# The lower halves of 56 weight chunks: by an accumulating transfer instead of a subtraction on VectorE

## The chip, the cores and the metric

The kernel runs on one core of one Trainium2 chip. The metric is the time on the device, in microseconds (us), of one execution of the program. Before the change the median of 3 runs is 1120.86 us (1120.05 to 1121.12).

## The reference

Two layers of a decoder trunk, on 512 tokens of 1024 channels, all in float32. Each layer norms its input, projects it with one matrix, and feeds four token mixers: A, attention over the 128 keys that an indexer selects for a query; B, a gated convolution over 3 tokens; C, stick-breaking attention; D, spatial gating in chunks of 128 tokens. The mixers' outputs are gated, projected, merged and projected once more:

```
h = rmsnorm(x, g_pre)
proj = h @ w_in                                   # (512, 1024) @ (1024, 8100)
a_q, a_k, a_v, a_iq, a_ik, a_iw, b_b, b_c, b_x, c_q, c_k, c_v, d_u, d_v, gate_paths, merge_logits = split(proj)
o = stack(A(...), B(...), C(...), D(...)) * silu(gate_paths)
z = einsum('bsnw,nwd->bsnd', o, w_branch)         # four of (512, 256) @ (256, 1024)
y = sum(sigmoid(merge_logits + b_merge) * z) @ w_out
x = x + rmsnorm(y, g_post)
x = x + (p_i @ w_ple) * sigmoid(x @ w_ple_gate)
```

## The kernel before

**Split operands.** Products of float32 are made of three products of float32r, a rounded form that TensorE multiplies at once. Each operand is kept as an upper half h (the value rounded to float32r) and a lower half l (the value less h), and `mm3` (L266) gives ah·bh + ah·bl + al·bh, three matmuls. So each weight has to be split before it is used.

**The weight stream.** The host lays all weights out as 180 chunks of up to 128 x 1024 in the order of their use, 90 for each layer (`chunk_plan`, L73). `load_to` (L231) issues their loads on SP's queue into three buffers named raw. `split_chunk` (L239) makes the halves: ScalarE casts raw into wh (L246), VectorE subtracts wh from raw into wl (L248), and then the load of the chunk three further on is issued, into the raw buffer that has come free. There are six buffers each of wh and wl (`WB`). Products name the operands by their buffers: `cc<-hh,wl` is a product of the lower half of a chunk of columns with the upper half of the normed input.

**Steps.** The work is a sequence of steps, one for each group of products: 164 in the plan, numbered through both layers. For each chunk the plan has the first and the last step of its use, and `split_steps` (L165) sets the step in which it is split: four steps ahead of its first use (`LEAD`), but not before the chunk whose buffer it takes has had its last use, and no more than one in a step. In the stages in which a step uses a chunk of its own this gives a lead of three or four steps; in the merges and in some output groups, where a step needs more than one buffer, it gives one or two.

**Order of the work.** A step goes round the jobs in hand: those that use the products of the step before (front), the split of this step, and the longer jobs (back: stick-breaking, gating, attention; idle: selection). A job gives way (HOP) where another engine goes on. Then come the step's products, and behind them the transposes and small products of the jobs that wait for TensorE. Each engine works through its queue in the order in which this writes it. From the projection of y to the first group of the next layer front jobs are issued ahead of the split (`chained`).

**The start** is written out by hand: the string `START` (L160) orders the first norm, its transposes, the splits of chunks 0 to 3 and the first group of products (steps 0 to 3). Behind it stand `make_tables` (sines, cosines), `make_masks`, and then the loop that splits what the plan puts before step 4:

```python
    make_tables()
    make_masks()
    ...
    while when[state["split"]][0] < 4:
        split_next()
    state["step"] = 4
```

By the plan these are chunks 4 and 5 (columns of the queries of mixer C), split in steps 0 and 1 and used in steps 4 and 5. `split_next` (L577) runs a split to its end without giving way. Step 4's products with chunk 4 (`cc`) are followed on TensorE by the transposes of mixer A's queries and keys (qktr, L455), from which ScalarE and VectorE make qT and kT.

**GpSimd** has little to do: two small loads at the start (posi, freq), masks, the power -0.5 of the norms (L443, L449), and the masking of scores (L857) and of the spatial weights (L1006). **At the turn of the layers** the last group of products (G1) finishes x for the next layer; its norm needs g_pre of that layer, which SP loads once the row buffer is free and its queue has come so far.

Of the kernel before, what the change touches and what calls it, by code (L numbers as in the profile page):

```python
# [50 lines left out]
# Weight chunks in the order of their use, each [128, 1024] or less.  "t": some tiles of 128 rows with all  # L51
# columns of a group (tokens on the partitions of the product); "c": all rows of 128 columns (columns on the
# partitions); "w": half of the columns of a branch's projection; "p": half of w_ple.
# [11 lines left out]
# groups that take two tiles of tokens through each half of the chunks  # L65
# [7 lines left out]
def chunk_plan():  # L73
    """(kind, elements of a partition, argument, first step, last step) of each chunk of each layer."""
    plan, step = [], 0
    for l in range(L):
        here = []

        def tgroup(name, cols, steps):
            nonlocal step  # L80
            n = tiles_of(cols)
            for c in range(KT // n):
                first, last = step, step + steps - 1
                if name in PAIRED and (l, name) != (0, "T1"):
                    first, last = step + c // 2, step + c // 2 + 2
                here.append(("t", n * cols, (name, c), first, last))
            step += steps

        def ccols(*names):
            nonlocal step  # L90
            for a in names:
                here.append(("c", KT * P, a, step, step))
                step += 1

        def both(n):
            return [(n, 0), (n, 1)]

        tgroup("T1", 512, 4)
        ccols(*both("cq"), *both("ck"))
        tgroup("CV", 256, 2)  # L100
        tgroup("T2", 420, 4)
        for c in range(2):
            ccols(("bc", c), ("bx", c), ("bb", c))
        ccols(*both("du"))
        tgroup("DV", 256, 2)
        for n in MERGES:
            ccols(*both(f"gate{n}"))
        for n in MERGES:
            for h in range(2):
                here.append(("w", 1024, (n, h), step, step + 3))  # L110
                ccols(*((f"merge{n}", dt) for dt in range(4 * h, 4 * h + 4)))
        for h in range(2):
            tgroup(f"Y{h}", 512, 4)
        for h in range(2):
            here.append(("p", 1024, h, step, step))
            step += 1
            tgroup(f"G{h}", 512, 4)
        plan.append(here)
    return plan
# [5 lines left out]
def lay_weights(w_in, w_branch, w_out, w_ple, w_ple_gate):  # L125
    parts = []

    def rows_in(a):
        """[n * 128, c] to [128, n * c]."""
        return a.reshape(-1, P, a.shape[1]).transpose(1, 0, 2).reshape(P, -1)  # L130
# [22 lines left out]
# buffers of each kind, and how many steps ahead of its use a weight chunk is split  # L153
QB, TB, SB, RAWB, WB, LEAD = 10, 25, 24, 3, 6, 4
# steps from the end of their operands to the stick-breaking heads, the selection and the attention, and the
# rounds of the selection in a step of B, D, the gates and the merges
STICKD, SELECT0, ATTEND0, RATES = 3, 8, 5, (1, 2, 3, 2)
# the start: sums of squares, norm, transposes, evacuation of a tile of tokens, split of the next weight chunk
# and products (of a tile of tokens with a chunk)
# [5 lines left out]
def split_steps(chunks):  # L165
    """The step in which each chunk is split in halves, and whether after the step's products."""
    out = []
    for k, (_, _, _, first, _) in enumerate(chunks):
        free = chunks[k - WB][4] if k >= WB else -2
        s = max(first - LEAD, free + 1, out[-1][0] if out else -1)  # L170
        if [o[0] for o in out].count(s) >= 1:
            s += 1
        s = min(s, first - 1)
        late = free >= s or bool(out) and out[-1] == (s, True)
        assert free <= s and (not out or out[-1] <= (s, late))
        out.append((s, late))
    return out
# [3 lines left out]
def hybrid_kernel(ctx: ExitStack, tc: tile.TileContext, w, x, p_t, pos, inv_freq, rows, small, ws_t, b_sp, out):  # L181
# [18 lines left out]
    def halves_cm(name):  # L200
        """Two split tiles of channels: (h, l), each [128, 2, 512]."""
        q = Q(name)
        return q[:, 0:2], q[:, 2:4]

    def halves_tm(name):
        """256 split columns of each tile of tokens: (h, l), each [128, 4, 256]."""
        q = Q(name).rearrange("p (a k) (b f) -> p a (k b) f", a=2, b=2)
        return q[:, 0], q[:, 1]

    def stacked(name):  # L210
        """256 columns of each tile of tokens, each head's 64 as their halves: [128, 4, 4, (h, l), 64]."""
        return Q(name).rearrange("p t (n a f) -> p t n a f", n=4, a=2)
# [17 lines left out]

    def load_to(i):  # L231
        while state["load"] < min(i, len(chunks)):
# [3 lines left out]
            load(raws[k][:, :n], bass.AP(tensor=w.tensor, offset=w.offset + offs[k], ap=[[n, P], [1, n]]))  # L236
            state["load"] += 1

    def split_chunk(k):  # L239
# [6 lines left out]
        A.copy(h[:, :n], r[:, :n])  # L246
        yield HOP
# [3 lines left out]
    def due(late):  # L251
        """The splits of this step."""
# [13 lines left out]
    def mm3(ps, a, b, start, stop):  # L266
        """ps += a.T b of two split operands."""
# [25 lines left out]
    # A job yields HOP where another engine goes on, PE before products that wait for what it has just told,  # L293
    # and STEP behind them.
# [3 lines left out]
    def rounds(live):  # L298
        """Goes round the jobs until each of them has ended or waits; those that wait for products."""
# [47 lines left out]
    def row(l, o, name):  # L347
        """1024 of rows, on every partition."""
# [31 lines left out]
    # key blocks of a unit, with the column at which each starts  # L380
# [37 lines left out]
    def make_masks():  # L418
# [4 lines left out]
        # -1 where row >= column  # L423
# [4 lines left out]
        # far below where the key (row) is not before the query (column)  # L428
# [6 lines left out]
    def rstd(v, parts, n):  # L435
        """v = (sum(parts) / n + eps) ** -0.5 of columns."""
# [8 lines left out]
    def rstd2(v, ss):  # L445
        """The same of two halves of which the first is divided and has eps."""
# [4 lines left out]
    def turn_blocks(name, src):  # L451
        """The four [128, 128] blocks of src, each transposed."""
# [23 lines left out]
    def weigh(out, v, j, n, wh, wl, start, stop):  # L476
        """The keys of block j by their weights: the halves of the values' products, one above the other."""
# [13 lines left out]
    def tgroup(lhs, cols, use, apart=None, finish=None):  # L491
        """Token-major products: use(t, psum) is the job that goes on with a tile of tokens.  With apart,
        two tiles at a time, the second job that many steps behind the first.  With finish, the
        last tile goes by halves of the columns: finish(t, psum, columns) is their job."""
# [24 lines left out]
    def tpairs(lhs, use):  # L519
        """The same for 256 columns, two tiles at a time."""  # L520
# [11 lines left out]
    def ccol(use):  # L532
        """Channel-major products of the normed input: use(psum) is the job that goes on."""
        k, = take()
        ps = bank("cc")
        step(lambda: cmm(ps, k))
        front.append(use(ps))
# [45 lines left out]
    # the first group of products takes tokens and weights as they come in  # L583
# [27 lines left out]
    for l in range(L):  # L611
# [29 lines left out]
        def use_t1(t, ps):  # L641
# [5 lines left out]
            # queries: the upper half and, on the other half of the partitions, the lower; keys: the upper  # L647
            # half twice, and the lower
# [24 lines left out]
        def use_cq(c, ps):  # L673
            """Queries of two heads: the upper half twice (on both halves of the partitions), and the lower."""
# [7 lines left out]
        def use_ck(c, ps):  # L682
            """Keys of two heads: the upper half and, on the other half of the partitions, the lower."""
# [11 lines left out]
        def stick(c, b):  # L695
# [11 lines left out]
            def smm(u):  # L707
                """Sums over the keys behind each key, without those of the later blocks in common()."""
# [5 lines left out]
            def sums(ps, first, blocks, own=None):  # L714
                """Sums of blocks of keys; of their own, over the later keys."""
# [6 lines left out]
            def common():  # L722
                """What the two last blocks of keys add to both of the first."""
# [71 lines left out]
        def use_t2(t, ps):  # L795
# [8 lines left out]
            # query halves (h, h, l) against key halves (h, l, h), stacked along the contraction  # L804
# [31 lines left out]
        def select():  # L836
            """bias[i]: 0 at the keys that each query of tile i keeps, far below at the others."""
# [35 lines left out]
        def attend():  # L873
            """Two tiles of queries and a head at a time; every round has a unit in each of four stages."""
# [5 lines left out]
            def blocks(m2):  # L880
                """(key block, tiles it is used by, column) of the transposed weights."""
# [200 lines left out]
        def use_merge(n, dt, ps, z):  # L1082
            """m += 2 sigmoid(..) (o w_branch): the half goes into the last step."""
# [93 lines left out]
        def project(hf):  # L1177
            """Half of p w_ple, in columns hf, and half of it."""
# [29 lines left out]
        def finish(t, ps, cs):  # L1208
            """Columns of the second half of the result."""
# [88 lines left out]
```

## Time and profile before

| | |
|---|---|
| median of 3 runs (lowest, highest) | 1120.86 us (1120.05, 1121.12) |
| span of the profiled execution, first to last instruction | 1118.6 us |
| its time as a whole | not listed apart from the span, which is 2.3 us below the median |
| TensorE products (PE), weight loads (PEld) | 1109.1 us (99%), 924.3 us (83%) |
| VectorE (DVE), ScalarE (ACT), GpSimd (POOL) | 760.5 us (68%), 492.6 us (44%), 23.7 us (2%) |
| read from HBM, written | 103.91 MB, 4.19 MB |

Times in the rows are microseconds from the start of the span unless marked ns. A product's name gives what is written and what is read, as `tg<-wl,hh`. "PE" rows are matmuls, "PEld" their weight loads, which run beside the matmuls before them; each matmul is listed until its result is out, so that successive ones overlap and the spacing of their starts is the pace. "<-" behind a time of idleness names what ended it.

### The profile page before, as it was taken

The numbers are of one execution on the slowest core, as the hardware profiler recorded it, in microseconds if no ns is written. First come the engines' busy times: TensorE is split into PE (matmuls) and PEld (weight loads), VectorE is DVE, ScalarE is ACT, GpSimd is POOL, SyncE is SP. The second block draws the span as 40 slices with busy tenths as digits, with TensorE's granted clock in tenths as the row PEclk, the third lists the DMA queues.
The fourth block names the chain that finished last, engine by engine and source line by source line (L and its number), as shares of the span: only waits on it lengthen the run. The fifth ranks groups of instructions, "written<-read, shape, count | busy, mean of one in ns | idle before, by whom it ended". The sixth has DMA issues, their size and how long they took to land.

```text
span 1118.6 us, 13984 instructions
## 1 busy us (share of the span) xinstructions
PE 1109.1 (99%) x5300; PEld 924.3 (83%) x5300; DVE 760.5 (68%) x1420; ACT 492.6 (44%) x857; POOL 23.7 (2%) x46
## 2 busy tenths in 40 slices
PE   8999999999999999999999999999999999999998
PEld 6888888888888888888788988988888888888887
DVE  5967769866788754547577677698668886454562
ACT  5566654323423433434446576433243244333341
POOL 2000000000000000000000000000000000000000
PEclk9999999999999999999999999999999999999999
DMA  5232232322233223542522222313222322226331
GB/s 193 84 109 76 76 99 58 113 76 76 76 94 94 76 90 99 170 151 95 166 97 81 78 74 76 100 61 111 82 86 71 99 76 76 95 94 205 114 114 38
DMA packets 34349, 109.01 MB, mean 97 GB/s; under 512 B 4057, under 2 KB 4841, under 8 KB 34282
## 3 DMA queue, kind: packets, MB, share of 16 engines
q1 hardware_dynamic: 34218, 108.10, 30.2%
q8 instruction: 41, 0.67, 0.2%
q0 software_dynamic: 64, 0.03, 0.1%
q14 instruction: 26, 0.21, 0.1%
HBM read 103.91 MB, written 4.19 MB: 97 GB/s over the span
## 4 chain that ended last, share of the span: by engine, by line
PE 95%; ACT 1%; DVE 1%; DMA 1%; issue 1%; SPq 0%; POOL 0%; DVEq 0%; ACTq 0%
PE mg L269 11%; PE mg L270 10%; PE mg L271 10%; PE tg L269 7%; PE tg L271 7%; PE tg L270 7%; PE cc L269 6%; PE cc L271 6%; PE cc L270 6%; PE z L270 3%; PE z L271 3%; PE z L269 3%; PE tp L270 1%; PE tp L269 1%; PE cs L719 1%; PE tp L271 1%
## 5 line engine op out<-in xcount | busy, mean ns | idle before, releaser
L248 DVE TENSOR_TENSOR wl<-raw,wh 128x1024 fp32r<-128x1024 f32 (+1 forms) x180 | 217.2, 1211 | 19.6 <-ACT wh L246 18.8
L269 PE MATMUL mg<-hh,wh 128*128 128x512 f32 x512 | 201.0, 392 | 0.0
L270 PE MATMUL mg<-hl,wh 128*128 128x512 f32 x512 | 199.4, 389 | 0.0
L271 PE MATMUL mg<-hh,wl 128*128 128x512 f32 x512 | 199.3, 389 | 0.0
L246 ACT CAST wh<-raw 128x1024 fp32r<-128x1024 f32 (+1 forms) x180 | 185.4, 1038 | 10.6 <-DMA raw<-in_w 4.1
L1085 ACT ACTIVATE g<-mg,prm 128x512 f32<-128x512 f32 x64 | 44.2, 690 | 231.0 <-PE mg L271 231.0
L269 PE MATMUL cc<-hh,wh 128*128 128x512 f32 x320 | 126.0, 394 | 0.0
L271 PE MATMUL cc<-hh,wl 128*128 128x512 f32 x320 | 124.8, 390 | 0.0
L270 PE MATMUL cc<-hl,wh 128*128 128x512 f32 x320 | 124.7, 390 | 0.0
L269 PEld LDWEIGHTS mg<-hh,wh 128*128 128x128 f32 x512 | 96.1, 188 | 21.9 <-issue 1.5
L271 PEld LDWEIGHTS mg<-hh,wl 128*128 128x128 f32 x512 | 96.1, 188 | 20.1
L270 PEld LDWEIGHTS mg<-hl,wh 128*128 128x128 f32 x512 | 96.1, 188 | 19.4
L1091 DVE SCALAR_TENSOR_TENSOR g<-g,z 128x512 f32<-128x512 f32 x48 | 32.9, 686 | 72.7 <-PE z L271 72.6
L271 PEld LDWEIGHTS cc<-hh,wl 128*128 128x128 f32 x320 | 60.1, 188 | 12.8
L269 PEld LDWEIGHTS cc<-hh,wh 128*128 128x128 f32 x320 | 60.1, 188 | 12.3 <-issue 0.7
L270 PEld LDWEIGHTS cc<-hl,wh 128*128 128x128 f32 x320 | 60.2, 188 | 11.6
L865 DVE MAX8 m<-cur 128x8 f32<-128x256 f32 (+2 forms) x96 | 53.6, 559 | 4.4 <-POOL cur L857 2.6
L866 DVE MATCH_REPLACE8 cur<-m,cur 128x256 f32<-128x256 f32 (+2 forms) x96 | 52.1, 543 | 0.0
L269 PE MATMUL tg<-wh,xh 128*128 128x512 f32 (+1 forms) x136 | 51.7, 380 | 0.0
L271 PE MATMUL tg<-wh,xl 128*128 128x512 f32 (+1 forms) x136 | 51.3, 377 | 0.0
L270 PE MATMUL tg<-wl,xh 128*128 128x512 f32 (+1 forms) x136 | 51.3, 377 | 0.0
L269 PE MATMUL tg<-wh,mh 128*128 128x512 f32 x128 | 50.0, 390 | 0.0
(251 smaller groups left out, 2019.5 us busy)
## 6 DMA issues: line engine op xcount, KB each, us to landing
raw<-in_w SPq DMA_DIRECT2D x172, 512.0 KB, 3.5
raw<-in_w SPq DMA_DIRECT2D x8, 420.0 KB, 3.1
x<-in_x SPq DMA_DIRECT2D x8, 256.0 KB, 5.6
res<-in_x SPq DMA_DIRECT2D x8, 256.0 KB, 4.3
xdram<-res SPq DMA_DIRECT2D x8, 256.0 KB, 3.5
res<-xdram SPq DMA_DIRECT2D x8, 256.0 KB, 5.6
out<-res SPq DMA_DIRECT2D x7, 256.0 KB, 2.1
gpost<-in_rows SPq DMA_DIRECT2D x2, 512.0 KB, 5.7
```

The lines of the kernel that those rows point to most:

```text
L246: A.copy(h[:, :n], r[:, :n])
L248: V.tensor_tensor(lo[:, :n], r[:, :n], h[:, :n].bitcast(F32), op=ALU.subtract)
L269: nc.tensor.matmul(ps, ah, bh, start=start, stop=False)
L270: nc.tensor.matmul(ps, ah, bl, start=False, stop=False)
L271: nc.tensor.matmul(ps, al, bh, start=False, stop=stop)
L719: nc.tensor.matmul(ps[:, (i - first) * P:], tri if i == own else ones, sh[u][q][:, ci:ci + S - i * P], start=(i == blocks[0] and q == 0), ...
L865: V.max(m8, cur[:, :n])
L866: V.match_replace(cur[:, :n], m8, cur[:, :n], TAKEN)
L1085: A.activation(g, ps, AF.Tanh, bias=b_merge(n, dt), scale=0.5)
L1091: V.scalar_tensor_tensor(g, g, 1.0, z, op0=ALU.add, op1=ALU.mult)
```

## The change

For a chunk whose planned first use is at least three steps behind its planned split, ScalarE, after the cast, writes the negated upper half into wl: a copy of raw with the factor -1, rounded as the cast rounds. GpSimd then issues a transfer that reads the chunk once more from HBM and adds it onto wl in place, so that wl holds raw - wh. VectorE has no part in it, and raw is free once ScalarE has read it. The condition holds for 56 of the 180 chunks: 4 and 5; in layer 1 numbers 14 to 22, 24 to 32, 76, 80, 81, 85 and 86; in layer 2 numbers 90, 91, 94 to 98, 100, 104 to 112, 114 to 122, 166, 170, 171, 175 and 176. All others are split as before. The address of a chunk in HBM gets a function of its own.

```diff
+    def chunk_at(k):
+        n = chunks[k][1]
+        return bass.AP(tensor=w.tensor, offset=w.offset + offs[k], ap=[[n, P], [1, n]])
+
     def load_to(i):
...
-            load(raws[k][:, :n], bass.AP(tensor=w.tensor, offset=w.offset + offs[k], ap=[[n, P], [1, n]]))
+            load(raws[k][:, :n], chunk_at(k))
             state["load"] += 1

     def split_chunk(k):
...
         r = raws.pop(k)
         A.copy(h[:, :n], r[:, :n])
+        if chunks[k][3] - when[k][0] >= 3:
+
+            A.mul(lo[:, :n], r[:, :n], -1.0)
+            yield HOP
+            nc.gpsimd.dma_start(lo[:, :n], chunk_at(k), accum_op=ALU.add)
+            load_to(k + 1 + RAWB)
+            return
         yield HOP
         V.tensor_tensor(lo[:, :n], r[:, :n], h[:, :n].bitcast(F32), op=ALU.subtract)
         load_to(k + 1 + RAWB)
```

## Rows read from the trace of the kernel before

**Rows 1.** The page: busy time of each engine; granted clock in 40 slices.

```profile
PE 1109.1 (99%) x5300; PEld 924.3 (83%) x5300; DVE 760.5 (68%) x1420; ACT 492.6 (44%) x857; POOL 23.7 (2%) x46
...
PEclk9999999999999999999999999999999999999999
```

**Rows 2.** All waits of TensorE's products: us in total, times, longest us.

```profile
PE gpre L359 <- DMA line<-in_rows: 2.4, 1, 2.4
PE htr L455 <- DVE h L566: 1.9, 2, 1.7
PE htr L455 <- DVE h L1248: 0.8, 1, 0.8
PE tp L270 <- DVE wl L248: 0.3, 1, 0.3
```

**Rows 3.** Groups of instructions by form: busy us, mean ns; idle us before them.

```profile
L248 DVE TENSOR_TENSOR wl<-raw,wh 128x1024 fp32r<-128x1024 f32 x172 | 209.1, 1219 | 19.5 <-ACT wh L246 18.8
...
L246 ACT CAST wh<-raw 128x1024 fp32r<-128x1024 f32 x172 | 178.3, 1044 | 10.6 <-DMA raw<-in_w 4.1 <-issue 3.5 <-PE tg L271 2.8
...
L279 ACT ACTIVATE mh<-m 128x512 fp32r<-128x512 f32 x16 | 10.1, 633 | 18.0 <-DVE m L1092 18.0
```

**Rows 4.** Timeline (start us, us), casts and first products of chunks 86, 98, 107.

```profile
528.06 1.04 ACT L246 CAST wh<-raw 128x1024 fp32r<-128x1024 f32 x1
...
541.63 0.39 PE L270 MATMUL tg<-wl,xh 128*128 128x512 f32 x1
...
600.98 1.04 ACT L246 CAST wh<-raw 128x1024 fp32r<-128x1024 f32 x1
...
613.31 0.28 PE L270 MATMUL tp<-wl,hh 128*128 128x256 f32 x1
...
651.23 1.05 ACT L246 CAST wh<-raw 128x1024 fp32r<-128x1024 f32 x1
...
676.93 0.39 PE L271 MATMUL cc<-hh,wl 128*128 128x512 f32 x1
```

**Rows 5.** Timeline of ScalarE, 33 to 46 us.

```profile
34.95 2.93 ACT L246 CAST wh<-raw 128x1024 fp32r<-128x1024 f32 x3
44.35 0.38 ACT L279 ACTIVATE qT<-qktr 64x256 fp32r<-64x256 f32 x1 [6.46 <-PE qktr L455]
```

**Rows 6.** Timeline of VectorE, 36 to 38 us.

```profile
36.21 2.35 DVE L248 TENSOR_TENSOR wl<-raw,wh 128x1024 fp32r<-128x1024 f32 x2
```

**Rows 7.** Timeline of TensorE, 38 to 44 us.

```profile
38.49 0.39 PE L270 MATMUL cc<-hl,wh 128*128 128x512 f32 x1
38.72 0.39 PE L271 MATMUL cc<-hh,wl 128*128 128x512 f32 x1
...
43.71 1.03 PE L455 MATMUL qktr<-ident,qkr 128*128 128x128 f32 x8
```

**Rows 8.** DMA issues: count, KB each, median us from issue to landing.

```profile
raw<-in_w SPq DMA_DIRECT2D x172, 512.0 KB, 3.5
...
freq<-in_inv_freq POOLq DMA_DIRECT2D x1, 24.0 KB, 5.5
...
posi<-in_pos POOLq DMA_DIRECT2D x1, 2.0 KB, 3.1
```

**Rows 9.** Stretches: us, busy us of PE, PEld, DVE, ACT, POOL; clock, DMA share, GB/s.

```profile
38.00:40.00 2.00, 2.00 (x10) 1.65 (x10) 1.97 (x5) 0.00 (x0) 0.00 (x0) 1.00 0.63 240
40.00:42.00 2.00, 2.00 (x11) 1.65 (x10) 1.97 (x5) 0.00 (x0) 0.00 (x0) 1.00 0.81 277
```

**Rows 10.** The chain that ended last (start us, us), 47 to 64 us.

```profile
47.43 0.38 ACT qT L279
...
62.52 1.24 DVE wl L248
63.80 0.39 PE tp L270
```

**Rows 11.** The chain that ended last, at the turn of the layers.

```profile
542.71 6.26 DMA gpre<-in_rows
```

**Rows 12.** The chain that ended last, 14 to 18 us.

```profile
15.35 0.43 PE tg L269
...
16.63 0.43 PE tg L269
...
17.32 0.23 PE tg L271
```

## The prediction

> **What bounds the kernel now.** I read the page first, then the waits of TensorE, then the chain and the timeline around the places where TensorE has no reserve. In the page TensorE is busy 99% of the span, VectorE 68%, ScalarE 44%, GpSimd 2% [rows 1]: the engine that the change relieves is not the one that sets the time. The waits of TensorE say it more sharply: over the whole span it waited four times for anything but its own work, 2.4 + 1.9 + 0.8 + 0.3 = 5.4 us together, and one of these, the 0.3 us, is for a lower half that VectorE had to write [rows 2]. Everything that VectorE does for the weights is hidden behind products already. So there is almost nothing to win, and the question is where the new way of making a lower half comes later than the old one.
>
> **The change, part by part.** *VectorE* loses 56 subtractions of 1219 ns, 68 us of work; *ScalarE* gains 56 scaled copies. A scaled copy of half that width takes 633 ns where it reads SBUF, and the plain cast of a whole chunk 1044 ns, so I take the cast's 1.04 us: 58 us more for ScalarE [rows 3]. On the path to the end the first is worth the waits that it ends, at most 0.3 + 0.8 us; I take nothing, as both waits stand behind chunks that are not among the 56 (9 and 89). The second is hidden at 54 places by ScalarE's own idle time and because the subtraction it replaces stood in VectorE's queue ahead of the same jobs; I take nothing, with an upper end of 1 us.
>
> *The lower half itself* now comes by a chain: cast, scaled copy, issue on GpSimd's queue, transfer, and only then the products. The condition for it is a lead of three steps in the plan. For 54 chunks the trace has room. I took, for each, the start of the first product with its lower half less the end of its cast less 1.04 us. The smallest is chunk 98's: the cast runs from 600.98 to 602.02, the first product with the half starts at 613.31, so 10.2 us remain; then chunk 86's, with a cast from 528.06 to 529.10, the product at 541.63, 11.5 us remaining. The other 52 have 12 us and more, the most chunk 107's, with a cast from 651.23 to 652.28 and a product at 676.93, 23.6 us [rows 4]. GpSimd's queue has hardly anything in it; its waits for other work (the masking of the spatial weights, the powers of the norms, the masking of scores) hold an issue up by a few us where the room is over 14 us. The SP queue's refills of the raw buffers now wait for ScalarE's copy instead of VectorE's subtraction, no later than now. Cost: nothing, as long as issue to landing stays below 10 us.
>
> *Chunk 4 has no such lead.* By the plan it is split in step 0 for step 4. But the first four chunks and the first steps are written out by hand, and chunks 4 and 5 are split in the loop behind the tables and the masks, just ahead of step 4. The timeline shows it: ScalarE casts chunks 4, 5 and 6 from 34.95 on, 0.95 us apart [rows 5]; VectorE subtracts for 4 and 5 from 36.21 to 38.56 [rows 6]; TensorE's third product of chunk 4, the first with the lower half, starts at 38.72 [rows 7]. The subtraction for chunk 4 is done 1.3 us ahead. With the change ScalarE does cast 4, copy 4, cast 5, copy 5, so copy 4 ends at about 36.95. The issue follows, and TensorE stands until the landing.
>
> How long an accumulating transfer takes no row shows. The nearest: the two that GpSimd issued, 2 KB landing after 3.1 us and 24 KB after 5.5 us, each with 0.5 to 0.7 us on GpSimd's queue, and the plain load of 512 KB from SP, 3.5 us [rows 8]. In the stretches in which the loads of chunks 7 and 8 run the DMA engines move 240 and 277 GB/s [rows 9], so that 0.52 MB takes 2.0 us of all 16. The lower end is the 2 KB transfer's 3.05 us with no time for the bytes: landing at 40.0, a stall of 1.3 us. The upper end is 5.5 us and three times 2.0 us (source, destination read again, and chunk 7's load, which the same end of copy 4 releases): landing at 48.4, a stall of 9.7 us. I take 3.05 + 2.0 for the source + 2.0 for one of the other two, since a transfer that reads what it writes can't be as short as a plain one: landing at 44.0, a stall of **5.3 us**. Chunk 5 is needed a step (24 products and 8 transposes, some 6.3 us) later than chunk 4 and lands about 2 to 4 us behind it: no second stall.
>
> The stall is passed on whole. The transposes of queries and keys stand behind chunk 4's products on TensorE (43.71) [rows 7], and ScalarE, idle 6.46 us before them [rows 5], runs without a break from there to the subtraction that TensorE waits for at 63.80 [rows 10]. Both engines shift together, and later no idle time of TensorE can take it back.
>
> *One more place*: at the turn of the layers the chain runs through the load of g_pre, issued at 542.71 and 6.26 us on its way [rows 11], for which TensorE waits 0.8 us in the end [rows 2]. Chunk 90's new transfer is issued at about 545, beside it. Bounds 0 and 2.0 us (one chunk's bytes); I take **1.0 us**, about half overlapping.
>
> The sum: 0 + 0 + 5.3 + 1.0 = +6.3 us. The profiled execution's span, 1118.6 us, lies 2.3 us below the median of the three runs, 1120.86 us; its own time apart from the span isn't listed. The sum is put on the median: **1127.2 us**, 0.56% slower. What lies within 0.2% (2.24 us) counts as no change, about what a measurement can tell here.
>
> **A rule against the rows.** By the rows a transfer from GpSimd takes 3.1 us with nearly no bytes [rows 8]. The Trainium skill (DMA: Bandwidth & Descriptors, Anatomy of one DMA — SWDGE (gpsimd) path) gives about 2.0 us plus the bytes over 436 GB/s for a whole transfer, an estimate of 3.2 us for 512 KB. By it the stall would be 1.4 us and the sum +2.4 us with g_pre's; the 2 KB row alone uses up that time, so I go by the rows. The forecast does without this.
>
> **The rivals.**
>
> *The transfer is nearly as quick as the quickest row.* At up to 3.9 us from issue to landing the stall is at most 2.2 us, and with no delay of g_pre the time is some 1122.5 us, no change. For it speaks the plain load of 3.5 us at the same size; against it that GpSimd's issue is the slower in the two rows there are, that the bytes go three ways, and that chunk 7's load goes at the same moment.
>
> *TensorE's clock falls in the stall.* At the start products came 0.43 us apart (its lower level, 1.2 GHz), after waits of up to 1.7 us [rows 2], until about 17 us [rows 12]; from then on 0.23 us [rows 7], with the granted clock at full in every slice [rows 1]. If 5 us of idleness brings the lower level back, the 22 products of chunk 4 still to come cost 0.2 us more each, 4.4 us on the same path: some 1131.6 us. Against it: the 0.8 us wait at 553 did nothing of the kind, and no row shows a long one. The Trainium skill (TensorE: Matmul & The Clock Gate, Part 1) says that an idle TensorE returns to half its clock; no stretch here shows it after the start.
>
> *The accumulation is slow throughout.* At 13 us from issue to landing chunk 4 stalls 11.3 us, chunk 98 some 2.8, chunk 86 some 1.5, a few others up to 1 each: about 1140 us, and with 16 us more than 1160, since then a dozen chunks are late. It decides from 10.2 us on [rows 4]. For it: an operation that the trace doesn't show at all; against: the DMA engines are used only 0.63 to 0.81 even while loads run [rows 9].
>
> *The other side*: VectorE's 56 subtractions read 2 x 512 KB each while TensorE reads its operands. If that slows TensorE's products, their absence speeds it: 56 steps of 24 products are 1344, and 1.7 ns each would be 2.3 us. If chunk 4 also found its half in time, some 1118.4 us. Against it: the spacing is 0.23 us whether VectorE subtracts or not, as at 38.49 and 38.72 [rows 7]. It decides from 1.7 ns a product, and with chunk 4's stall it would need far more.
>
> **How the numbers follow.** Forecast (stall of 2.3 to 10 us, clock stays) 0.52; clock falls too 0.20; slow accumulation 0.10; quick landing 0.12; faster 0.06. Slower: 0.52 + 0.20 + 0.10 = 0.82; same 0.12; faster 0.06. The range starts at the quick landing (+1.3, 1122) and reaches to the upper ends of the forecast (+9.7 + 2.0, 1132.6) and of the clock's fall behind it (+4.4): 1122 to 1137. Outside lie the faster case and the slow accumulation.
>
> **What would show it.** In the changed kernel's waits of TensorE a new row should stand: the weight load or product of cc with wl at about 38.5 us, released by the DMA of wl from in_w, of some 5 us, and hardly any other such wait. The page should give VectorE about 692 us and ScalarE about 551 us, and HBM reads 29 MB more. The stretch from 43.7 to 63.8 should be shifted, not longer. The wait for h at the turn of the layers should have grown from 0.8 us to some 1.8 us. Wrong would be: no stall at 38.5 us (landing under 3 us), many stalls at wl (landing over 10 us), products 0.43 us apart behind the stall, or a TensorE that waits for ScalarE in the branch steps.

## The result, and the profile after

The changed kernel takes 1131.45 us (median of 4 runs, 1130.39 to 1132.82) against 1120.95 us for the kernel before on the same chip: ratio 1.0097 [1.0083, 1.0112], some 10.5 us or 1% slower. The span of the profiled execution went from 1118.6 to 1129.3 us.

The page of the changed kernel: busy time of each engine, the granted clock, the queues of the DMA engines (q1 takes the issues of SP, q0 those of GpSimd; packets, MB, share of 16 engines' span), and the two new groups (busy us, mean ns, idle before).

```profile
PE 1110.7 (98%) x5300; PEld 924.6 (82%) x5300; DVE 698.9 (62%) x1364; ACT 545.2 (48%) x913; POOL 68.8 (6%) x102
...
PEclk9899999999999999999999999999999999999999
...
q1 hardware_dynamic: 34218, 108.10, 30.9%
q0 software_dynamic: 8128, 29.30, 14.4%
...
HBM read 133.18 MB, written 4.19 MB: 122 GB/s over the span
...
L255 POOL DMA_DIRECT2D wl<-in_w x56 | 48.8, 871 | 706.4 <-ACT wl L253 452.3
...
L253 ACT ACTIVATE wl<-raw 128x1024 fp32r<-128x1024 f32 (+1 forms) x56 | 59.1, 1056 | 0.0
```

Against [rows 1], VectorE has 62 us less and ScalarE 53 us more, and HBM reads 29.3 MB more. One digit of the granted clock is no longer a 9. TensorE's busy time has grown by 1.6 us only, so the rest of the 10.7 us is waiting. The waits of TensorE (us in total, times, longest us) say where:

```profile
PE cc L282 <- DMA wl<-in_w: 7.0, 1, 7.0
PE gpre L370 <- DMA line<-in_rows: 2.4, 1, 2.4
PE htr L466 <- DVE h L1259: 1.8, 1, 1.8
PE htr L466 <- DVE h L577: 1.5, 2, 1.2
PE tg L280 <- ACT hh L288: 1.5, 1, 1.5
PE tp L281 <- DVE wl L259: 0.3, 1, 0.3
```

Beside [rows 2] there are two new rows. One is a single wait of 7.0 us for a lower half that comes by DMA. The other, 1.5 us for the upper half of the normed input (hh), lies at 10.8 us, ahead of everything that the change touches; it varies between profiles, and the last kernel below, which has nothing of the change, shows it with 0.3 us. The wait at the turn of the layers has gone from 0.8 to 1.8 us. Not one of the other 55 transfers appears. The chain that ended last (start us, us) passes through the new wait:

```profile
37.70 8.60 DMA wl<-in_w
46.31 0.04 issue
46.35 0.80 PE cc L282
47.15 0.43 PE cc L280
47.57 0.43 PE cc L281
...
49.70 0.43 PE cc L280
50.13 0.24 PE cc L281
50.37 0.23 PE cc L282
```

Chunk 4's transfer is issued at 37.70 and lands at 46.31, and the product that started at 38.72 before [rows 7] starts at 46.35. Behind it successive products are 0.43 us apart for a while and then 0.23. The same stretch by windows of 2 us (busy us and count of PE, PEld, DVE, ACT, POOL; granted clock; DMA share; GB/s) shows what that is:

```profile
38.00:40.00 2.00, 1.33 (x6) 0.75 (x4) 1.96 (x5) 2.00 (x3) 1.04 (x2) 1.00 0.74 229
40.00:42.00 2.00, 0.00 (x0) 0.00 (x0) 1.97 (x3) 0.23 (x1) 0.47 (x1) 1.00 0.81 100
42.00:44.00 2.00, 0.00 (x0) 0.00 (x0) 1.97 (x5) 0.00 (x0) 0.00 (x0) 0.80 1.02 242
44.00:46.00 2.00, 0.00 (x0) 0.00 (x0) 1.80 (x4) 0.00 (x0) 0.00 (x0) 0.50 1.05 281
46.00:48.00 2.00, 1.65 (x4) 1.36 (x5) 0.00 (x0) 0.00 (x0) 0.00 (x0) 0.50 1.05 272
48.00:50.00 2.00, 2.00 (x6) 1.52 (x6) 0.00 (x0) 0.00 (x0) 0.00 (x0) 0.50 0.62 186
50.00:52.00 2.00, 2.00 (x10) 1.65 (x9) 0.00 (x0) 0.00 (x0) 0.00 (x0) 0.99 0.00 0
```

While TensorE has nothing to do the granted clock falls to 0.50, the lower level of 1.2 GHz, and it stays there until about 50 us. In [rows 9] the windows from 38 to 42 us had TensorE busy throughout at 1.00.

**Where the 10.7 us went.** Both kernels have the same 5300 products in the same order, so the difference in the start of each product can be followed through the span. It is 0.45 us ahead of the stall (from the first products, before any change acts). The stall adds 7.18 us and the slow products behind it 1.86 us. Then the difference stays where it is, to 0.02 us, through some 500 us; the turn of the layers adds 1.02 us and the rest of the span 0.15 us. The sum is 10.7 us.

### The profile page after: what moved, and what is told of

Its sections match the earlier page's. It is cut to its first block, busy times and chain, and to the rows that moved or that the text cites. A ratio compares the mean times of both kernels' runs of the same rounds, so it can differ in the third digit from the quotient of the medians.

```text
span 1129.3 us, 14077 instructions
## 1 busy us (share of the span) xinstructions
PE 1110.7 (98%) x5300; PEld 924.6 (82%) x5300; DVE 698.9 (62%) x1364; ACT 545.2 (48%) x913; POOL 68.8 (6%) x102
## 3 DMA queue, kind: packets, MB, share of 16 engines
q1 hardware_dynamic: 34218, 108.10, 30.9%
q0 software_dynamic: 8128, 29.30, 14.4%
## 4 chain that ended last, share of the span: by engine, by line
PE 93%; ACT 2%; DMA 1%; DVE 1%; issue 1%; POOL 0%; SPq 0%; DVEq 0%; POOLq 0%; ACTq 0%
PE mg L280 11%; PE mg L281 10%; PE mg L282 10%; PE tg L280 7%; PE tg L281 7%; PE tg L282 7%; PE cc L280 6%; PE cc L282 6%; PE cc L281 6%; PE z L282 3%; PE z L281 3%; PE z L280 3%; PE tp L281 1%; PE tp L280 1%; PE cs L730 1%; PE tp L282 1%
## 5 line engine op out<-in xcount | busy, mean ns | idle before, releaser
L259 DVE TENSOR_TENSOR wl<-raw,wh 128x1024 fp32r<-128x1024 f32 (+1 forms) x124 | 149.4, 1209 | 29.8 <-ACT wh L250 29.5
L255 POOL DMA_DIRECT2D wl<-in_w x56 | 48.8, 871 | 706.4 <-ACT wl L253 452.3
L253 ACT ACTIVATE wl<-raw 128x1024 fp32r<-128x1024 f32 (+1 forms) x56 | 59.1, 1056 | 0.0
```

What stands on the lines that cost most here:

```text
L253: A.mul(lo[:, :n], r[:, :n], -1.0)
L255: nc.gpsimd.dma_start(lo[:, :n], chunk_at(k), accum_op=ALU.add)
L259: V.tensor_tensor(lo[:, :n], r[:, :n], h[:, :n].bitcast(F32), op=ALU.subtract)
```

## The experiments

Each kernel below ran on one chip beside the kernel before, and its ratio is to that. Their profiles differ by up to 2.3 us in what the start of the program takes ahead of chunk 4 (from 0.7 us less than in the profile of before to 1.6 us more), so stalls are read from the difference of products within a profile, and times from the medians. A time given as so much under the changed kernel's goes across chips, on which the kernel before took 1120.7 to 1121.2 us.

**Chunks 4 and 5 by VectorE, the other 54 by transfer.** Is the whole loss in those two?

```diff
-        if chunks[k][3] - when[k][0] >= 3:
+        if chunks[k][3] - when[k][0] >= 3 and k not in (4, 5):
```

> Chunks 4 and 5 are split by VectorE again, the other 54 of the 56 stay with the transfer. If the loss sits at chunk 4 (stall and what follows it on TensorE, 9.1 us) and at the turn of the layers (1.0 us), 1.0 to 1.5 us above the kernel before: about 1122, ratio 1.001, and no wait of TensorE for a transfer. If instead the 54 others cost something all along the way (more DMA traffic, ScalarE's 57 us more), several us stay: 1124 or more.

Measured: 1121.55 us, ratio 1.0006 [0.9997, 1.0015]. No wait for a transfer is left; the wait at the turn of the layers is 1.2 us. So 54 transfers cost nothing that this measurement can tell, and the 66 us of subtractions that VectorE no longer does (54 of 1219 ns, [rows 3]) bring nothing either. Nor do a cost and a gain cancel: from chunk 4 on, the start of each product against the kernel before changes by 0.6 us in all, 0.45 us of it at the turn of the layers.

**The same, and chunk 90 by VectorE too** (it is split at the turn of the layers, beside the load of g_pre).

```diff
+        if chunks[k][3] - when[k][0] >= 3 and k not in (4, 5, 90):
```

> As the kernel with 54, and chunk 90 too by VectorE (53 by transfer). If chunk 90's transfer is what holds up the load of g_pre, TensorE's wait for h at the turn is 0.8 us again, and the time is that of the kernel before, 1121.0 (within 0.5 us). If other transfers or ScalarE's copies hold it up (chunk 86's), the wait stays near 1.8 us and the time at about 1122.

Measured: 1120.92 us, ratio 1.0002 [0.9992, 1.0011]; the wait at the turn is 1.0 us. That is 0.2 us from the 0.8 us of the one reading and 0.2 us from the kernel with 54, so the run does not say whether chunk 90's transfer is what held up g_pre.

**Only chunks 4 and 5 by transfer.**

```diff
-        if chunks[k][3] - when[k][0] >= 3:
+        if k in (4, 5):
```

> Only chunks 4 and 5 by transfer, the other 178 by VectorE. If the loss sits at chunk 4, 9.1 us above the kernel before, about 1130, with a stall of 7 us at 38.9 us and products 0.43 us apart behind it, and a wait of 0.8 us at the turn. If the 54 others carry a part, less: 1126 or below.

Measured: 1130.69 us, ratio 1.0088 [1.0073, 1.0103]: nearly the whole loss with 2 of the 56. TensorE waits 7.1 us at chunk 4, and the slow products behind it cost 2.5 us; the turn of the layers adds 0.46 us instead of 1.02.

**TensorE kept busy through the wait**: 30 extra products of chunk 4's upper half ahead of its own, whose result the real ones overwrite.

```diff
-        step(lambda: cmm(ps, k))
+        def mm():
+            if k == 4:
+                for _ in range(30):
+                    nc.tensor.matmul(ps, halves[k][0][:, :P], hT[0][0][:, 0], start=True, stop=True)
+            cmm(ps, k)
+        step(mm)
```

> The changed kernel with 30 more products (upper half of chunk 4 by the input, into the bank that chunk 4's first product then overwrites) ahead of chunk 4's, 6.8 us of work in place of idleness. If the slower products behind the stall come from TensorE's idleness, the clock stays at its upper level, the wait for the transfer shrinks to about 0.5 us, and 1.9 us come back: about 1129.5 against 1131.4. If they come from something else (the transfer's traffic), the products behind stay 0.43 us apart and the time stays at 1131.4.

Measured: 1129.75 us, ratio 1.0076 [1.0059, 1.0093], 1.7 us under the changed kernel's median. The windows of this kernel over the wait:

```profile
42.00:44.00 2.00, 2.00 (x10) 1.67 (x9) 1.97 (x5) 0.00 (x0) 0.00 (x0) 1.00 0.97 236
44.00:46.00 2.00, 1.99 (x9) 1.31 (x7) 1.61 (x4) 0.00 (x0) 0.00 (x0) 1.00 1.07 279
46.00:48.00 2.00, 0.59 (x3) 0.50 (x4) 0.00 (x0) 0.00 (x0) 0.00 (x0) 1.00 1.03 268
48.00:50.00 2.00, 2.00 (x10) 1.67 (x9) 0.00 (x0) 0.00 (x0) 0.00 (x0) 1.00 0.42 150
```

The clock stays at 1.00, and the products are 0.23 us apart as soon as the half is there. What is left of the wait is 1.4 us, until the landing at 47.4 us, where 0.5 us was expected: the transfer took 9.8 us here. The idleness of TensorE is what takes the clock down. The two intervals overlap, so it is the windows that show this, and the 1.7 us agree with it.

**Chunks 4 and 5 by a plain transfer.** GpSimd copies the chunk instead of adding it, so the lower halves of these two hold the raw chunk; that part of mixer C's queries is changed.

```diff
-            nc.gpsimd.dma_start(lo[:, :n], chunk_at(k), accum_op=ALU.add)
+            if k in (4, 5):
+                nc.gpsimd.dma_start(lo[:, :n], chunk_at(k))
+            else:
+                nc.gpsimd.dma_start(lo[:, :n], chunk_at(k), accum_op=ALU.add)
```

> Chunks 4 and 5 still go through GpSimd's queue, but their transfer copies the chunk instead of adding it, so the lower halves of these two hold the raw chunk (that part of the products of mixer C's queries is changed, the work is the same). Theory (adding is what makes it slow: its 4 KB packets take some 330 ns against 150 to 170 of a load): landing about 1.5 to 2.5 us earlier than the 46.3 us of the changed kernel, a stall at chunk 4's first lower-half product of 4.7 to 5.7 us instead of 7.2, time 1.5 to 3 us under the changed kernel's. Rival (issue on GpSimd and the loads beside it set it): landing at 46 us or later, a stall of 7 us, the same time as the changed kernel's 1131.5.

Measured: 1127.39 us, ratio 1.0060 [1.0046, 1.0073], 4.1 us under the changed kernel. Issue to landing is 4.7 us (37.79 to 42.47) instead of 8.6, and the wait 3.1 us, both below what the theory gave. So adding costs 3.9 us at this place, with the loads beside it. In the packet records between issue and landing a packet of 4 KB takes 0.19 us on average, and 0.40 us in the changed kernel. TensorE's timeline (start us, us) behind the wait is worth a look:

```profile
42.52 0.50 PE L285 MATMUL cc<-hh,wl 128*128 128x512 f32 x1 [3.05 <-DMA wl<-in_w]
42.85 0.39 PE L283 MATMUL cc<-hh,wh 128*128 128x512 f32 x1
43.08 0.39 PE L284 MATMUL cc<-hl,wh 128*128 128x512 f32 x1
43.31 0.47 PE L285 MATMUL cc<-hh,wl 128*128 128x512 f32 x1
43.58 0.63 PE L283 MATMUL cc<-hh,wh 128*128 128x512 f32 x1
44.01 0.63 PE L284 MATMUL cc<-hl,wh 128*128 128x512 f32 x1
...
46.57 0.55 PE L284 MATMUL cc<-hl,wh 128*128 128x512 f32 x1
46.96 0.40 PE L285 MATMUL cc<-hh,wl 128*128 128x512 f32 x1
47.20 0.39 PE L283 MATMUL cc<-hh,wh 128*128 128x512 f32 x1
```

The products come back at 0.23 us, and a microsecond later, with TensorE at work, they go to 0.43 us until 47 us. The fall cost 1.8 us, as much as behind the wait of 7.0 us.

**The loads of chunks 7 and 8 not issued by the splits of 4 and 5.**

```diff
-            load_to(k + 1 + RAWB)
+            if k not in (4, 5):
+                load_to(k + 1 + RAWB)
```

> The ends of the splits of chunks 4 and 5 no longer issue the loads of chunks 7 and 8; these come with chunk 6's, some us later. Theory (half of the time above an undisturbed 5.9 to 6.3 us is the loads beside it): landing about 1 to 2.4 us earlier, a stall of 4.8 to 6.2 us, time 1129 to 1130.5. Rival (loads do not matter, as their queue shares the engines evenly and the engines are not full): landing within 0.5 us of 46.3, stall 7 us, time 1131.5.

Measured: 1130.88 us, ratio 1.0091 [1.0076, 1.0107], a wait of 7.4 us. But the kernel did not do what it was to do, as the timeline of SP's queue shows:

```profile
37.00 4.78 SPq L221 DMA_DIRECT2D raw<-in_w  x3
```

The loads go as early as in the changed kernel: there it is at 37.42 us, in a profile in which chunk 4's products start 0.42 us later than in this one. SP holds nothing but loads; moved back in the program, they wait for the same thing as before, the raw buffer that ScalarE has read. The run says nothing on crowding; the next but two does.

**Chunk 4's lower-half products last**: the 16 with its upper half first, then the 8.

```diff
+        if k == 4:
+            for a in range(3):
+                for kt in range(KT):
+                    nc.tensor.matmul(ps, (h, h, lo)[a][:, kt * P:(kt + 1) * P], hT[kt // 4][(0, 1, 0)[a]][:, kt % 4],
+                                     start=a == 0 and kt == 0, stop=a == 2 and kt == KT - 1)
+            return
```

> Chunk 4's 16 products with its upper half first, the 8 with its lower half last: 14 products (3.2 us) more stand ahead of the wait. Theory (the stall is the landing less the moment at which TensorE needs it): a wait of 3.8 to 4.3 us at about 42 us, ended at the same 46 us; time 3.2 us under the changed kernel's if the clock falls as far as there, 5 us under it (1126.5) if a wait of 4 us leaves the clock at full. Rival (TensorE's products slow the transfer, by the operands they read): landing later by what is hidden, a stall of 5 us or more, time within 2 us of the changed kernel's.

Measured: 1127.84 us, ratio 1.0063 [1.0050, 1.0077], 3.6 us under the changed kernel. The wait is 4.3 us, ended at the same 46.1 us, and products behind it are 0.43 us apart to the end of the chunk: the clock fell. The products with the lower half and the eight transposes behind them lost 2.6 us by it; 0.4 us of that came back where the other kernels wait for a lower half once more (at 63.80 us in the kernel before, [rows 10]) and this one does not. What the order hides of the stall is gained, and no more.

**The 54 transfers, with the load of g_pre issued ahead of the second half of the ple projection.**

```diff
...
+            if hf and more:
+                nxt["gpre"] = row(l + 1, 0, "gpre")
             project(hf)
             if hf and more:
-                nxt["gpre"] = row(l + 1, 0, "gpre")
                 new_hT()
```

> The 54 transfers without chunks 4 and 5, and the load of g_pre issued ahead of the step of the second half of the ple projection. Theory (the wait at the turn of the layers is g_pre's landing, 1.2 us with the 54 transfers in the earlier run of them): the wait for h at the turn goes to 0 to 0.3 us, time 1120.3 to 1120.7, 0.8 to 1.2 us under that run's 1121.55. Rival (another wait takes its place, the norm's sums or VectorE's queue): the wait for h stays at 0.8 us or more, time 1121 to 1122.

Measured: 1120.64 us, ratio 0.9998 [0.9990, 1.0007]. The wait at the turn is gone altogether, and the first transposes behind it come 0.94 us earlier, relative to the products ahead of them, than in the kernel before. So g_pre's landing is what TensorE waited for there. Its 0.9 us is at the edge of what the time can tell.

**The loads held back in fact.** A late reader on VectorE (a copy of one column of each of the raw buffers of chunks 4, 5 and 6) keeps the buffers in use.

```diff
-        r = raws.pop(k)
+        r = held[k] = raws.pop(k)
...
-            load_to(k + 1 + RAWB)
+            if k not in (4, 5, 6):
+                load_to(k + 1 + RAWB)
...
+            if k == 4:
+                for c in (4, 5, 6):
+                    V.tensor_copy(scr[:, c:c + 1], held[c][:, :1])
+                load_to(10)
+            cmm(ps, k)
...
```

> The raw buffers of chunks 4 to 6 get a late reader on VectorE (a copy of one column each, behind the ropes of step 4), so that the loads of chunks 7, 8 and 9 cannot start before about 46 us. Chunk 5's transfer still runs beside chunk 4's. Theory (an undisturbed transfer lands 5.9 to 6.3 us after its issue, and the 2 to 3 us above it for chunk 4 come from the loads and from chunk 5's transfer about equally): landing 7 to 7.8 us after issue, a stall of 5.5 to 6.4 us, time 1130 to 1131. Rival (the loads take nothing from it): 8.6 to 9 us after issue, stall 7.2 us, 1131.5.

Measured: 1127.50 us, ratio 1.0060 [1.0046, 1.0074]. The chain of this kernel:

```profile
37.66 5.54 DMA wl<-in_w
43.20 0.04 issue
43.24 0.50 PE cc L284
43.74 0.23 PE cc L282
...
44.20 0.24 PE cc L284
44.44 0.43 PE cc L282
...
47.43 0.42 PE cc L283
47.85 0.23 PE cc L284
```

SP issued the loads at 41.95, earlier than I had said, but their first packets came at 44.9, behind the landing. Issue to landing is 5.5 us instead of 8.6: the loads cost chunk 4's transfer all of the 3.1 us, and both theories were wrong on the size. VectorE was busy 1.96 us or more of every 2 us from 38 to 44 us, as in the changed kernel, so it isn't a quieter VectorE. The packet records say how the loads cost it. Between issue and landing an adding packet of 4 KB takes 0.39 us on average without the loads and 0.40 with them, so the packets themselves are no slower. But without the loads the first one starts 1.6 us after the issue instead of 2.4, and from there to the landing it is 3.9 us instead of 6.2; the loads that run in these 6.2 us take 1.7 us of all 16 engines.

**The same, and chunk 5 by VectorE**, so that chunk 4's transfer is alone.

```diff
-        if chunks[k][3] - when[k][0] >= 3:
+        if chunks[k][3] - when[k][0] >= 3 and k != 5:
...
```

> The same, and chunk 5 by VectorE: chunk 4's transfer has the DMA engines to itself. Theory (crowding): landing 5.9 to 6.5 us after issue, as the undisturbed ones, a stall of 4.5 to 5.2 us; the clock still falls, as it does behind a wait of 3.1 us, for some 1.8 us; time 1128 to 1129.3. Rival (the first transfer is slow by itself, as its first packets of 660 to 920 ns suggest): 8 us or more after issue, stall of 6.6 us or more, time above 1130.5.

Measured: 1128.02 us, ratio 1.0060 [1.0046, 1.0073]. Issue to landing is 5.6 us (37.86 to 43.42), as with chunk 5's transfer behind it: that one, issued 1.9 us later on the same queue, did not hold up the one ahead. Landing and wait (4.0 us) came a little under what the theory gave. The clock fell and cost 1.5 us. The first packets are slow here too (0.85 us at 39.5), so that is no sign of crowding.

**All 56, with the splits of chunks 4 and 5 ahead of the tables.**

```diff
+    while when[state["split"]][0] < 4:
+        split_next()
     make_tables()
     make_masks()
...
-    while when[state["split"]][0] < 4:
-        split_next()
```

> All 56 by transfer, but the splits of chunks 4 and 5 stand ahead of the tables and the masks, where ScalarE is idle from 28.7 to 32.8 us: issues at about 30.8 and 32.7 instead of 37.7 and 39.6. Theory (the stall is the missing lead and nothing else): landing at 37 to 39.5 us, a wait for the lower half of at most 0.8 us, no fall of the clock, time 1121.0 to 1122.5, as the 54 alone. Rival (the tables, now later by 1 to 2 us behind ScalarE's casts and GpSimd's issues, or the transfer itself in the crowded start, delay something else): a wait of 2 us or more at another place, time 1124 or more.

Measured: 1122.82 us, ratio 1.0017 [1.0008, 1.0026]. Its waits of TensorE:

```profile
...
PE htr L466 <- DVE h L1259: 1.6, 1, 1.6
PE cc L282 <- DMA wl<-in_w: 1.2, 1, 1.2
...
```

The issue comes at 29.72 and the half is there at 39.4, 9.6 us later, with loads beside it from 29.44 on. So 8 us more of lead take 6 of the 7 us, and the clock stays at 1.00. Wait and time came out a little above what the theory gave (0.8 us, 1122.5), though the landing lies within its 37 to 39.5 us: in this profile TensorE reached chunk 4's products 0.7 us earlier than in the kernel before. The tables delay nothing: behind chunk 4 the difference to the kernel before stays within 0.02 us up to the turn of the layers.

**The kernel before, with g_pre's load first** (the edit of the run with 54 transfers, without the change).

> The kernel of before with the load of g_pre issued ahead of the step of the second half of the ple projection. Theory (the 0.8 us wait at the turn of the layers is its landing): the wait goes to 0 to 0.3 us, time 0.5 to 0.8 us under the kernel of before, ratio 0.9993 to 0.9996, under what a measurement can tell. Rival (another wait behind it): wait of 0.6 us or more, ratio 1.000.

Measured: 1119.35 us, ratio 0.9987 [0.9978, 0.9996], the only version that is faster than the kernel before. All waits of TensorE in it:

```profile
PE htr L455 <- DVE h L566: 3.2, 2, 2.9
PE gpre L359 <- DMA line<-in_rows: 2.3, 1, 2.3
PE tp L270 <- DVE wl L248: 0.3, 1, 0.3
PE tg L269 <- ACT hh L277: 0.3, 1, 0.3
```

The row for h at L1248 of [rows 2] is gone. Products behind the turn come 0.94 us earlier; the median says 1.8 us with an interval of 0.4 to 2.5 us, so 0.9 is what is shown by rows and the rest is not accounted for.

## Why the prediction was right, and where it was not

Forecast 1127.2 us in a range from 1122 to 1137; measured 1131.45. Direction, place and mechanism were right: one stall at chunk 4's first lower-half product, passed on whole, and next to nothing elsewhere. Two terms were off, each by 1.9 us, and together they are nearly all of the 4.3 us that the forecast fell short.

**VectorE and ScalarE at nothing: right.** Busy times came out at 698.9 and 545.2 us, where 692 and 551 were given. The runs with 54 and 53 transfers lie at 1.0006 [0.9997, 1.0015] and 1.0002 [0.9992, 1.0011]; a gain of 2.3 us, as in the rival on the other side, would be 0.998. (With chunk 4 in time that rival's sum is 1118.6 us, not 1118.4.) TensorE's pace is 0.23 us with and without VectorE's subtractions: the difference of products to the kernel before holds to 0.02 us through some 500 us.

**The 54 transfers with a lead at nothing: right, with less to spare than the medians suggest.** The DMA issues of the changed kernel (count, KB each, median us to landing):

```profile
raw<-in_w SPq DMA_DIRECT2D x172, 512.0 KB, 3.7
wl<-in_w POOLq DMA_DIRECT2D x55, 512.0 KB, 7.8
```

They take from 5.9 to 10.5 us to land, 7.8 us at the median; the longest is chunk 5's. Chunks 98 and 86, named in the prediction as the tightest, had 2.5 and 2.6 us to spare when their halves were needed. The rival of a slow accumulation would have begun at 10.2 us of issue and landing at chunk 98; it took 7.5 us there.

**Chunk 4's stall: right mechanism, size 7.2 us where 5.3 were taken** (bounds 1.3 and 9.7). The term that was mis-sized is the landing's sum, 3.05 + 2.0 for the source + 2.0 "for one of the other two". Counted from the end of ScalarE's copy, that gave 7.05 us; measured are 0.3 us to the issue and 8.6 us to the landing. What the sum lacked is the loads. Without them the transfer lands 5.5 us after issue, 5.8 us from the copy's end; with them it lands 3.1 us later. I had put them down as chunk 7's alone and as either-or with the destination; in the trace about 1.1 MB of loads move between issue and landing, twice one chunk, and both of "the other two" are due. For a transfer without loads the sum was 1.2 us too long (7.05 against 5.8), and which of its three terms was too long is not shown, as no plain transfer ran without loads. By the packets the destination's term was about right: an adding packet takes 0.2 us more than a plain one, and 128 of them over 16 engines make an estimate of 1.7 us. The quick landing is out: even the plain transfer takes 4.7 us.

The Trainium skill (DMA: Bandwidth & Descriptors, Anatomy of one DMA — SWDGE (gpsimd) path) would give an estimate of 3.2 us for this size; the rows here differ, with 4.7 us for the plain transfer among loads and 5.5 us for the accumulating one alone. The Trainium skill (DMA: Bandwidth & Descriptors, Queues, rings and completion order) says that each DMA engine goes round its queues packet by packet, by which loads in another queue would lengthen a transfer; 5.5 us against 8.6 us agrees.

**The clock: a rival at 0.20 that came true beside the likeliest case, at 1.9 us of the 4.4 given.** The likeliest case was written with a clock that stays, and it did not. The evidence "against" was a wait of 0.8 us that does nothing; that it was no evidence for a wait of 5 us stood in the same sentence, and I weighed it too lightly. The price was an upper bound for all 22 products left; eight or nine were slow. The runs show no fall after waits of 1.2 and 1.4 us at chunk 4 and of up to 1.8 us at the turn of the layers; after waits of 3.1, 3.9, 4.0, 4.3, 7.0, 7.1 and 7.4 us they show a fall that costs 1.5 to 2.6 us with no order by length.

The Trainium skill (TensorE: Matmul & The Clock Gate, Part 1) says that an idle TensorE drops to half its clock; the 0.50 in the windows and the 0.43 us between products agree, and the run with the busy TensorE, at 1.00 throughout, agrees too.

**The turn of the layers: 1.0 forecast, 1.02 in the changed kernel's profile.** Over all runs with chunk 90 by transfer, and g_pre's load where it was, the turn adds 0.3 to 1.0 us, and over two without it 0.2 and 0.5 us. So perhaps half of the 1.0 us is the transfer's, and the two groups overlap: that the forecast was met to 0.02 us is luck. That g_pre's landing is behind the wait is shown by the two runs that issue it earlier; the prediction's other account of this wait, behind the split of chunk 89, is out.

**Of the signs named ahead**, the new wait, the reads (29.3 MB where 29 were given), the shift without a stretch and the wait of 1.8 us for h were there; "products 0.43 us apart behind the stall", put down as a sign against the forecast, was there as well.

What stays open, beside the terms of the landing: whether TensorE's own reading slows a transfer. With 30 extra products beside it chunk 4's took 9.8 us, with 14 more of its own products 9.1, with neither 8.6 to 9.0; the differences are no larger than those between transfers elsewhere.

## What to carry to other kernels

A lead that a plan promises is worth only what the program gives it: look in the trace of before for the time between the producer's end and the first use at every place where the new path is taken, the hand-written start above all, because one place with 1.3 us of reserve lost here what 54 places could not bring. Where an engine that isn't the bound is relieved, expect no more than the waits on it that end, and price the new path with the other transfers that run at its moment, not by its size alone. Where TensorE is the bound, a stall can cost more than its length: here stalls of 3 to 7 us cost some 2 us of lower clock on top.

## What the runs showed of the hardware

**Adding in a transfer is dear.** By the page of the changed kernel GpSimd's queue used 14.4% of 16 engines' span for 29.3 MB and SP's 30.9% for 108.1 MB: times 1129.3 us, 5.6 us of all engines for a MB against 3.2, a factor of 1.7. In the packet records of the changed kernel the median accumulating packet of 4 KB takes 0.33 us, the median packet of a load 0.16 us.

**The clock can fall after the wait is over.** In the run with the plain transfer, TensorE had been at work again for a microsecond, at 0.23 us a product, when the products went to 0.43 us, and the run with the loads held back shows the same behind its wait of 3.9 us (43.24 to 44.44). In the changed kernel the clock was down before the wait ended. The price was the same, 1.8 us against 1.9: shortening the stall from 7 to 3 us saved the stall's difference and nothing of the clock's.

**Loads moved back in the program need not start later.** SP's loads moved back in the program went out at the same moment, 37.0 us against 37.42 in a profile that lies 0.42 us behind; only a later release of their buffers held them back, to 41.95 us.
